# A transformer layer on one core: the residual stream moves from SBUF to the output in DRAM, and four of five down-projection parts are added to it by accumulating transfers

## The chip, the cores and the metric

The kernel runs on one core of a Trainium2 chip, in float32. Its engines work side by side, each through its own queue in order: TensorE (PE, with its weight loads as PEld), VectorE (DVE), ScalarE (ACT), GpSimd (POOL) and SyncE (SP), which here only issues transfers. The metric is the time of one execution on the device, in microseconds. Before the change it is 1356.28 us, the median of three runs (1355.2 to 1356.44).

## The reference

The kernel computes one encoder layer for 256 tokens of 2048 channels. What matters here is its second half:

```python
    x = x + (g[:, :, 0] * y_a + g[:, :, 1] * y_b) @ w_o

    gt, up = jnp.split(rms_norm(x, g_ffn) @ w_gate_up, 2, axis=-1)
    return x + (jax.nn.silu(gt) * up) @ w_down
```

The first line adds the attention branches to the residual stream `x`. The last one adds the feed-forward network (FFN) to it; its inner width is 5632. The result, 256 x 2048 float32 (2 MB), is the output.

## The kernel before

Every weight is read once from DRAM, in chunks. A chunk in the FFN is 1 MB, loaded by two transfers of 512 KB from SP's queue into one of three buffers (`x`, pool `xp`). It is split into two float32r parts: ACT casts it (`wh`, L220) and DVE subtracts the cast from the original (`wl`, L221). `wh` and `wl` live in six buffers, so three chunks of the FFN. PE then makes three products for each pair of tiles (`mm3`, L427 to L429). SP's next load into an `x` buffer waits until DVE has made `wl` of the chunk that held it; ACT's next cast waits until PE has freed a `wh` buffer. So a delay of one load can travel round this ring: load, cast, subtraction, next load.

The FFN goes by five parts of the inner width (`PARTS`, L40), numbered 0 to 4; the first has three column groups of 512, the others two. In each part:

- **Gate and up.** A column group takes eight chunks (`Quad`). Three of the eight are "fast" (L837): DVE and ACT make extra splits and sums of them (`rh`, `rl`, `r`, and the four additions L844 to L847, which write into the `x` buffer before its own cast and subtraction), and PE then needs seven products where it would need eight. At a group's end DVE collects four PSUM banks, A to D (`evac_fast` L658, `evac_pair` L670; L679 is the step that PE waits for before it writes bank C again).
- **Down.** Four column blocks of 512, j = 0 to 3, each 256 x 512, collected in the banks A, B, C and A. Blocks 0 and 1 run interleaved, then 2 and 3. When a block is complete, `evac_down` (L701) adds it to the residual tile `x1[j]`.

`x1[0]` to `x1[3]` are SBUF tiles of [128, 2, 512] float32 (512 KB each), made by `evac_wo` (L637) as the sum of the attention projection and the input. They are held from there to the end, 28 buffers of this size (pool `tp`) being shared with all other tiles of that size. After part 4 each goes to the output by one transfer from SP; the last block, j = 3, by halves and quarters as its rows are done (`evac_last`, L708).

The order of all instructions is written out by hand as far as the second block of `w_o`. From `ffn_at - 2` (L981) a list scheduler orders each engine's queue by the order of the code as a priority and its own costs. Functions registered with `at(group, fn, ahead)` (L932) run some steps ahead of that group's first product; `load_xres` is one.

Weight chunks are numbered through the program: 253 to 260 are the eight of part 1's first group; 255, 257 and 259 are its fast ones.

Of the kernel before, what the change touches and what calls it, by code (L numbers as in the profile page):

```python
# [15 lines left out]
ALU = mybir.AluOpType  # L16
# [3 lines left out]
P = 128  # L20
S = 256
NT = S // P
# [17 lines left out]
PARTS = ((0, 3), (3, 5), (5, 7), (7, 9), (9, 11))  # L40
# [55 lines left out]
def layer_kernel(ctx: ExitStack, tc: tile.TileContext, a: dict, out: bass.AP):  # L96
    nc = tc.nc
# [11 lines left out]
    def t4(shape, name, dt=F32):  # L109
        return tp.tile(shape, dt, name=name, tag="t4")  # L110

    def small(shape, name):
        return cp.tile(shape, F32, name=name)
# [30 lines left out]
    od = out[0].rearrange("(t p) d -> p t d", p=P)  # L144
# [50 lines left out]
    def rstd_of(ss, d, name):  # L195
        n = math.prod(ss.shape[1:])
        v = small(list(ss.shape), name + "_v")
        r = small(list(ss.shape), name)
        nc.gpsimd.tensor_scalar(v, ss, 1.0 / d, EPS, op0=ALU.mult, op1=ALU.add)
        flat = (lambda z: z) if len(ss.shape) == 2 else (lambda z: z.rearrange("p a b -> p (a b)"))  # L200
        nc.gpsimd.tensor_tensor(flat(r), flat(v), mhalf[:, :n], op=ALU.pow)
        return r
# [401 lines left out]
    x1, hP, hjobs, xres = {}, {}, {}, {}  # L604
    ss2 = small([P, NT, 4], "ss2")

    def load_xres(j):
        xres[j] = t4([P, NT, 512], f"xres{j}")
        nc.sync.dma_start(xres[j], xd[:, :, j * 512:(j + 1) * 512])
# [3 lines left out]
    def job_h(i):  # L613

        ps = half_side(f"tr_h{i}").rearrange("p (k s) -> p k s", s=S)
        for k in range(2):
            f = 2 * i + k
            for t in range(NT):
                nc.tensor.transpose(ps[:, k, t * P:(t + 1) * P], x1[f // 4][:, t, (f % 4) * P:(f % 4 + 1) * P], ident)
        g = [gain("g_ffn", 2 * i + k) for k in range(2)]  # L620
        if i not in FAST:
            hP[i] = t4([P, 2, 2, S], f"hP{i}", F32R)
            split_evac(*((hP[i][:, 0, k], hP[i][:, 1, k], ps[:, k], g[k]) for k in range(2)))
        else:
            v, l, h = t4([P, 8, P], f"hs{i}"), t4([P, 7, P], f"hsl{i}", F32R), t4([P, 7, P], f"hsh{i}", F32R)
            nc.scalar.activation(v[:, 0:8:7], ps[:, 0].rearrange("p (t s) -> p t s", t=NT), AF.Copy, scale=g[0])
            nc.scalar.activation(v[:, 1:3], ps[:, 1].rearrange("p (t s) -> p t s", t=NT), AF.Copy, scale=g[1])
            nc.vector.tensor_sub(v[:, 3], v[:, 7], v[:, 2])
            nc.vector.tensor_sub(v[:, 4], v[:, 7], v[:, 0])
            nc.vector.tensor_sub(v[:, 5], v[:, 0], v[:, 3])  # L630
            nc.vector.tensor_sub(v[:, 6], v[:, 1], v[:, 5])
            split_pair(h, l, v[:, :7])
            hq[i] = (h, l)
        return
        yield

    def evac_wo(j):  # L637
        def evac(ps, step):
            x1[j] = t4([P, NT, 512], f"x1_{j}")
            nc.vector.tensor_add(x1[j], ps, xres[j])  # L640
            sq = t4([P, NT, 512], f"sq1_{j}")
            for t in range(NT):
                nc.scalar.activation(sq[:, t], x1[j][:, t], AF.Square, accum_out=ss2[:, t, j:j + 1])

            for i in (2 * j, 2 * j + 1):
                hjobs[i] = Job(job_h(i))
                hjobs[i].ready = step + 2
                jobs.append(hjobs[i])
            if j == 3:
                s = small([P, NT], "ss2s")  # L650
                nc.vector.tensor_reduce(s, ss2, axis=AX.X, op=ALU.add)
                st["2"] = rstd_of(s, DM, "r2")
        return evac
# [46 lines left out]

    def evac_down(half, j):  # L701
        def evac(ps, step):
            nc.vector.tensor_add(x1[j], ps, x1[j])
            if half == len(PARTS) - 1:
                nc.sync.dma_start(od[:, :, j * 512:(j + 1) * 512], x1[j])
        return evac

    def evac_last(ps, t):  # L708
        for c in range(t + 1):
            w = 512 // (t + 1)  # L710
            s = slice(w * c, w * (c + 1))
            nc.vector.tensor_add(x1[3][:, t, s], ps[:, s], x1[3][:, t, s])
            (nc.scalar if c else nc.sync).dma_start(od[:, t, 1536 + w * c:1536 + w * (c + 1)], x1[3][:, t, s])
# [41 lines left out]
    for half, (j0, j1) in enumerate(PARTS):  # L755
        js = range(j0, j1)
        hidT[half] = Act(f"hid{half}", 4 * len(js))
        for i, j in enumerate(js):
            needs = {k: (lambda k=k: [hjobs[k]]) for k in range(NPAIR)}
            needs[FAST[0]] = lambda: list(hjobs.values())  # L760
            if i:
                needs[FAST[0]] = lambda half=half, i=i: [djobs[half, i - 1]]
            groups.append(Group(W["w_gate_up"], 512 * j, 1024, range(NPAIR), None, evac_pair(half, i, i == len(js) - 1), needs))
        for j in range(4):
            wd = W["w_down"][js[0] * 512:(js[-1] + 1) * 512]
            groups.append(Group(wd, 512 * j, 512, range(4 * len(js)), hidT[half], evac_down(half, j),
                                {k: (lambda k=k, half=half: [djobs[half, k // 4]]) for k in range(4 * len(js))}))
# [126 lines left out]
    def products(i):  # L894
        c, ks, first, last = steps[i]
        g, gi, allks, q = chunks[c]
        if q:
            return products_quad(c)
        final = gi == len(groups) - 1
        if first and gi < ffn_at:  # L900
            ps = psm.tile([P, NT, 512], F32, name=f"g{gi}", tag="main")
            gps[gi] = [ps, ps[:, 0], ps[:, 1]]
        elif first:
            ps = held[DOWN[g.c0 // 512]]
            gps[gi] = [ps, ps[:, 0], ps[:, 1]]
        ps = gps[gi]
        h, l = parts[c]
        if ks[-1] == allks[-1]:
            del parts[c]

        def products_of(t, k):
            ah, al = g.lhs(k)
            n, s = k - allks[0], slice(t * P, (t + 1) * P)
            mm3(ps[1 + t][:, :g.n], ah[:, s], al[:, s], h[:, n, :g.n], l[:, n, :g.n], k == g.ks[0], k == g.ks[-1])

        if final and last:
            for t in range(NT):
                for k in ks:
                    products_of(t, k)
                evac_last(ps[1 + t], t)  # L920
        else:
            for k in ks:
                for t in range(NT):
                    products_of(t, k)
        return ps[0]
# [3 lines left out]
    def gidx(fn_name, nth=0):  # L929
        return [i for i, n in enumerate(names) if f".{fn_name}." in n][nth]  # L930

    def at(gi, fn, ahead=8):  # L932
        early.setdefault(max(0, first_step[gi] - ahead), []).append(fn)
# [9 lines left out]
    for j in range(4):  # L943
        at(gidx("evac_g0", j), lambda j=j: load_bias(j))
        at(gidx("evac_g1", j), lambda j=j: load_bias(4 + j))
        at(gidx("evac_wo", j), lambda j=j: load_xres(j))

    after_evac = {}
    after_evac[gidx("evac_b", 0)] = lambda: jobs.append(prep["kr"])
    after_evac[gidx("evac_b", 6)] = lambda: limited.extend(attn["dil", p] for p in range(4))  # L950
# [28 lines left out]
    for i, (c, ks, first, last) in enumerate(steps):  # L979
# [18 lines left out]
        ps = products(i)  # L998
# [61 lines left out]
```

## Time and profile before

| | us |
|---|---|
| median of three runs | 1356.28 |
| the profiled execution, its own time | 1356.11 |
| its span (first to last instruction) | 1354.3 |
| time outside the span | 1.8 |

The profile is taken from one execution on the core. Its page gives busy times of the engines, the chain of work that ended last, and groups of equal instructions. A row of the timeline gives start, duration, engine, line, operation, what it writes and reads with its shape, and in brackets the idle time of the engine before it and what ended that. The stages by the clock of this trace: attention and its projections up to about 640 us; part 0 of the FFN to 830; parts 1 to 4 about 130 us each, with gate and up first and the down blocks in the last 43 us of each; the end at 1354.

### The profile page before, as it was taken

Reading aid. Unit: us, or ns where it says so; the run is one execution under the profiler, and the core shown is the slowest. Engines: PE = TensorE matmul, PEld = TensorE weight load, DVE = VectorE, ACT = ScalarE, POOL = GpSimd, SP = SyncE. Lnnn points to the kernel's source line nnn. Section 1 sums busy time; section 2 is a strip of 40 time slices with the busy share of each in tenths; the row PEclk is TensorE's granted clock in tenths of the full one; section 3 lists DMA queues with packets and bytes.
Section 4 is the critical chain, followed back from the end, with each engine's and each line's share of the span. In section 5 each row is a group of like instructions: output and inputs, shape, how many; then the busy total and the mean of one; then the engine's idle time right before and its main releaser. Section 6 shows DMA issues by size and latency. Waiting matters only on the chain.

```text
span 1354.3 us, 16169 instructions
## 1 busy us (share of the span) xinstructions
PE 1339.5 (99%) x6243; PEld 1126.0 (83%) x6243; DVE 949.1 (70%) x949; ACT 652.2 (48%) x724; POOL 34.3 (3%) x41
## 2 busy tenths in 40 slices
PE   8999999999999999999999999999999999999998
PEld 6899999988888888888788888888878888888886
DVE  5566777677645655567789756886798579857973
ACT  6455555454444444455455434454445345534541
POOL 1011112000000000000000000000000000000000
PEclk9999999999999999999999999999999999999999
DMA  7555555656556766676546665565457654754662
GB/s 247 179 175 161 161 170 167 184 161 176 174 186 205 212 188 202 209 235 207 201 158 213 221 187 183 191 213 190 157 185 245 191 186 172 229 190 163 214 214 93
DMA packets 138205, 257.14 MB, mean 190 GB/s; under 512 B 9192, under 2 KB 28688, under 8 KB 138128
## 3 DMA queue, kind: packets, MB, share of 16 engines
q1 hardware_dynamic: 137760, 255.96, 58.9%
q8 instruction: 49, 0.80, 0.2%
q14 instruction: 28, 0.23, 0.1%
q10 hardware_dynamic: 144, 0.13, 0.0%
q0 software_dynamic: 224, 0.01, 0.0%
HBM read 253.97 MB, written 2.10 MB: 189 GB/s over the span
## 4 chain that ended last, share of the span: by engine, by line
PE 94%; DVE 2%; issue 1%; DMA 1%; ACT 1%; SPq 0%; DVEq 0%; ACTq 0%
PE g L429 14%; PE g L427 14%; PE g L428 13%; PE sC L427 6%; PE sC L429 6%; PE sC L428 6%; PE mA L427 4%; PE mA L429 4%; PE mA L428 4%; PE sD L429 4%; PE sD L427 4%; PE sD L428 4%; PE mB L428 3%; PE mB L429 3%; PE mB L427 3%
## 5 line engine op out<-in xcount | busy, mean ns | idle before, releaser
L220 ACT CAST wh<-x 128x1024 fp32r<-128x1024 f32 (+3 forms) x349 | 465.3, 1352 | 437.0 <-DVE x L847 127.7
L221 DVE TENSOR_TENSOR wl<-x,wh 128x2048 fp32r<-128x2048 f32 x132 | 300.8, 2289 | 134.5 <-ACT wh L220 132.7
L221 DVE TENSOR_TENSOR wh<-x,wh 128x1024 fp32r<-128x1024 f32 (+2 forms) x217 | 250.6, 1172 | 113.1 <-ACT wh L220 111.9
L427 PE MATMUL g<-wh,xTh 128*128 128x512 f32 (+1 forms) x544 | 210.6, 387 | 0.6 <-ACT xTh L212 0.6
L429 PE MATMUL g<-wh,xTl 128*128 128x512 f32 (+1 forms) x544 | 207.9, 382 | 0.6 <-DVE xTl L217 0.6
L428 PE MATMUL g<-wh,xTh 128*128 128x512 f32 (+1 forms) x544 | 207.9, 382 | 0.0
L429 PEld LDWEIGHTS g<-wh,xTl 128*128 128x128 f32 x544 | 102.8, 189 | 17.6 <-DVE xTl L217 1.4
L427 PEld LDWEIGHTS g<-wh,xTh 128*128 128x128 f32 x544 | 102.8, 189 | 15.9 <-ACT xTh L212 0.9
L428 PEld LDWEIGHTS g<-wh,xTh 128*128 128x128 f32 x544 | 102.9, 189 | 15.4 <-DVE wh L221 0.4
L427 PE MATMUL sC<-wh,hP 128*128 128x512 f32 x220 | 86.1, 391 | 1.6 <-DVE u L679 1.5
L429 PE MATMUL sC<-wh,hP 128*128 128x512 f32 x220 | 85.7, 390 | 0.0
L429 PE MATMUL sD<-wh,hP 128*128 128x512 f32 x220 | 85.7, 389 | 0.0
L428 PE MATMUL sC<-wl,hP 128*128 128x512 f32 x220 | 85.7, 389 | 0.0
L427 PE MATMUL sD<-wh,hP 128*128 128x512 f32 x220 | 85.7, 389 | 0.0
L428 PE MATMUL sD<-wl,hP 128*128 128x512 f32 x220 | 85.7, 389 | 0.0
L220 ACT CAST rh<-x 128x1024 fp32r<-128x1024 f32 x33 | 34.7, 1051 | 36.1 <-DMA x<-in_w_gate_up_dram 36.1
L427 PEld LDWEIGHTS sC<-wh,hP 128*128 128x128 f32 x220 | 41.3, 188 | 12.3 <-issue 4.0
L427 PE MATMUL g<-wh,mTh 128*128 128x512 f32 x128 | 50.5, 394 | 0.0
L429 PE MATMUL g<-wh,mTl 128*128 128x512 f32 x128 | 49.9, 390 | 0.0
L428 PE MATMUL g<-wh,mTh 128*128 128x512 f32 x128 | 49.9, 390 | 0.0
L427 PEld LDWEIGHTS sD<-wh,hP 128*128 128x128 f32 x220 | 41.3, 188 | 8.6
L428 PEld LDWEIGHTS sD<-wl,hP 128*128 128x128 f32 x220 | 41.3, 188 | 8.6
(675 smaller groups left out, 2390.7 us busy)
## 6 DMA issues: line engine op xcount, KB each, us to landing
x<-in_w_gate_up_dram SPq DMA_DIRECT2D x176, 512.0 KB, 4.7
x<-in_w_down_dram SPq DMA_DIRECT2D x88, 512.0 KB, 5.0
x<-in_w_in_dram SPq DMA_DIRECT2D x79, 512.0 KB, 4.2
x<-in_w_in_dram SPq DMA_DIRECT2D x56, 448.0 KB, 3.6
x<-in_w_o_dram SPq DMA_DIRECT2D x32, 512.0 KB, 4.4
x<-in_w_o_mla_dram SPq DMA_DIRECT2D x16, 512.0 KB, 4.9
x<-in_w_o_dil_dram SPq DMA_DIRECT2D x16, 512.0 KB, 4.6
x<-in_w_ukv_dram SPq DMA_DIRECT2D x8, 512.0 KB, 4.0
```

Of the source, the lines that this page charges most:

```text
L220: nc.scalar.copy(h, x)
L221: nc.vector.tensor_sub(l, x, f32(h))
L427: nc.tensor.matmul(ps, ah, bh, start=first, stop=False)
L428: nc.tensor.matmul(ps, ah, bl, start=False, stop=False)
L429: nc.tensor.matmul(ps, al, bh, start=False, stop=last)
```

## The change

The residual stream is stored to the output in DRAM as soon as it is made. In the parts 0 to 3, ACT copies a finished down block from PSUM to a new SBUF tile `y`, and a transfer issued by POOL adds that tile to the output's columns in DRAM (`accum_op=ALU.add`). For part 4, the sum so far is read back from the output into new tiles `x1[j]` two steps ahead of each block's first product; the addition on DVE and the store are then as before.

```diff
@@ evac_wo
             for t in range(NT):
                 nc.scalar.activation(sq[:, t], x1[j][:, t], AF.Square, accum_out=ss2[:, t, j:j + 1])
 
+            nc.sync.dma_start(od[:, :, j * 512:(j + 1) * 512], x1[j])
             for i in (2 * j, 2 * j + 1):
@@ evac_down
         def evac(ps, step):
-            nc.vector.tensor_add(x1[j], ps, x1[j])
-            if half == len(PARTS) - 1:
-                nc.sync.dma_start(od[:, :, j * 512:(j + 1) * 512], x1[j])
+            cols = od[:, :, j * 512:(j + 1) * 512]
+            if half < len(PARTS) - 1:
+                y = t4([P, NT, 512], f"y{half}_{j}")
+                nc.scalar.copy(y, ps)
+                nc.gpsimd.dma_start(cols, y, accum_op=ALU.add)
+            else:
+                nc.vector.tensor_add(x1[j], ps, x1[j])
+                nc.sync.dma_start(cols, x1[j])
         return evac
+
+    def load_x1(j):
+        x1[j] = t4([P, NT, 512], f"x1b_{j}")
+        nc.sync.dma_start(x1[j], od[:, :, j * 512:(j + 1) * 512])
...
+    for j in range(4):
+        at(gidx("evac_down", 4 * (len(PARTS) - 1) + j), lambda j=j: load_x1(j), 2)
```

In the changed kernel the new lines are 645 (store of `x1`), 707 and 708 (copy and accumulating transfer), 710 and 711 (addition and store of part 4), 716 (read back); the four additions L844 to L847 stand at L854 to L857.

The scheduler also moves some instructions. On PE nothing moves but three products of part 0's first group, by a few places each. On ACT and DVE the same thing happens at the start of each of the parts 1 to 4. First ACT, where part 0's last down blocks meet part 1's first chunks, before:

```order
L220 CAST wh252_6303<-x252_6245 128x2048
L220 CAST wh253_6334<-x253_6276 128x2048
L220 CAST rh255_6366<-x255_6338 128x1024
L220 CAST r255_6368<-x255_6338 128x512
L220 CAST wh254_6377<-x254_6307 128x2048
L220 CAST wh255_6409<-x255_6338 128x2048
L220 CAST rh257_6440<-x257_6413 128x1024
L220 CAST wh256_6451<-x256_6381 128x2048
```

and in the change:

```order
L220 CAST wh253_6342<-x253_6284 128x2048
L220 CAST wh254_6387<-x254_6315 128x2048
L707 COPY y0_2_6373<-sC_5121 128x1024
L220 CAST rh255_6376<-x255_6346 128x1024
L220 CAST r255_6378<-x255_6346 128x512
L707 COPY y0_3_6418<-mA_5119 128x1024
L220 CAST wh255_6421<-x255_6346 128x2048
L220 CAST rh257_6452<-x257_6425 128x1024
L220 CAST wh256_6463<-x256_6391 128x2048
L220 CAST r257_6454<-x257_6425 128x512
```

Two copies have come in, and the cast of chunk 254 now stands ahead of the first two casts of chunk 255. DVE at the same place, before (`sC` and `mA` are the banks with the blocks 2 and 3):

```order
L221 TENSOR_TENSOR wl253_6335<-x253_6276,wh253_6334 128x2048
L221 TENSOR_TENSOR rl255_6367<-x255_6338,rh255_6366 128x1024
L703 TENSOR_TENSOR x1_2_4917<-sC_5117,x1_2_4917 128x1024
L221 TENSOR_TENSOR r255_6368<-x255_6338,r255_6368 128x512
L221 TENSOR_TENSOR wl254_6378<-x254_6307,wh254_6377 128x2048
L844 TENSOR_TENSOR x255_6338<-x255_6338 128x512
L845 TENSOR_TENSOR x255_6338<-x255_6338 128x512
L703 TENSOR_TENSOR x1_3_5097<-mA_5115,x1_3_5097 128x1024
L846 TENSOR_TENSOR x255_6338<-x255_6338 128x512
L847 TENSOR_TENSOR x255_6338<-x255_6338 128x512
L221 TENSOR_TENSOR wl255_6410<-x255_6338,wh255_6409 128x2048
```

and in the change:

```order
L221 TENSOR_TENSOR wl253_6343<-x253_6284,wh253_6342 128x2048
L221 TENSOR_TENSOR wl254_6388<-x254_6315,wh254_6387 128x2048
L221 TENSOR_TENSOR rl255_6377<-x255_6346,rh255_6376 128x1024
L221 TENSOR_TENSOR r255_6378<-x255_6346,r255_6378 128x512
L854 TENSOR_TENSOR x255_6346<-x255_6346 128x512
L855 TENSOR_TENSOR x255_6346<-x255_6346 128x512
L856 TENSOR_TENSOR x255_6346<-x255_6346 128x512
L857 TENSOR_TENSOR x255_6346<-x255_6346 128x512
L221 TENSOR_TENSOR wl255_6422<-x255_6346,wh255_6421 128x2048
```

The two additions are gone, and the subtraction of chunk 254 (`wl254`) has moved ahead of the two of chunk 255 (`rl255`, `r255`). On SP's queue, where part 4's down weights begin, stood before:

```order
L826 DMA x339_9335<-in_w_gate_up_dram 128x2x512 x2
L826 DMA x340_9374<-in_w_gate_up_dram 128x2x512 x2
L835 DMA x341_9405<-in_w_down_dram 128x2x512 x2
L835 DMA x342_9433<-in_w_down_dram 128x2x512 x2
L835 DMA x343_9464<-in_w_down_dram 128x2x512 x2
L835 DMA x344_9499<-in_w_down_dram 128x2x512 x2
L835 DMA x345_9538<-in_w_down_dram 128x2x512 x2
```

and now:

```order
L836 DMA x340_9410<-in_w_gate_up_dram 128x2x512 x2
L716 DMA x1b_0_9496<-out_0_dram 128x2x512
L845 DMA x341_9441<-in_w_down_dram 128x2x512 x2
L845 DMA x342_9469<-in_w_down_dram 128x2x512 x2
L845 DMA x343_9502<-in_w_down_dram 128x2x512 x2
L845 DMA x344_9537<-in_w_down_dram 128x2x512 x2
L716 DMA x1b_1_9572<-out_0_dram 128x2x512
L845 DMA x345_9578<-in_w_down_dram 128x2x512 x2
```

Each read back stands between two weight loads, and waits there for the accumulating transfers into its columns.

## The prediction

> **What bounds the kernel now.** I read the page's first and fourth parts, then the waits of PE alone from 640 us on (the FFN), then one window.
>
> ```profile
> PE 1339.5 (99%) x6243; PEld 1126.0 (83%) x6243; DVE 949.1 (70%) x949; ACT 652.2 (48%) x724; POOL 34.3 (3%) x41
> PE 94%; DVE 2%; issue 1%; DMA 1%; ACT 1%; SPq 0%; DVEq 0%; ACTq 0%
> ...
> PE sD L691 <- DVE z L685: 1.7, 2, 1.0
> PE sC L427 <- DVE u L679: 1.5, 5, 0.9
> PE mA L619 <- ACT hs L627: 0.9, 1, 0.9
> PE mA L427 <- DVE x L712: 0.8, 1, 0.8
> ...
> 520.00:640.00 120.00, 120.00 (x551) 99.59 (x550) 76.11 (x78) 60.31 (x77) 0.00 (x0) 1.00 0.65 214
> ```
>
> PE is busy for 99% of the span and carries 94% of the last chain. In the whole FFN its waits sum to 4.9 us, and between 520 and 640 us, where the residual is made, it is busy in all 120.00 us. The change takes no matmul away. So the forecast starts from 1356.11 us, the profiled execution's own time (0.17 us under the median of the runs shown, which is nothing beside the terms below). To gain, the change must remove one of these waits; to lose, it must make a new one.
>
> **The change part by part.** The 16 additions of parts 0 to 3 leave DVE, and 16 copies of the same shape come to ACT.
>
> ```profile
> L703 DVE TENSOR_TENSOR x<-mA,x 128x1024 f32<-128x1024 f32 x9 | 11.0, 1221 | 7.0 <-PE mA L429 7.0
> L210 ACT CAST hid1h<-sD 128x1024 fp32r<-128x1024 f32 x1 | 1.0, 1018 | 0.3 <-PE sD L691 0.3
> ```
>
> DVE loses 16 x 1.22 = 19.5 us. ACT, by its nearest row (the same shape from PSUM, 1.02 us), gains 16.3 us. Both engines have room (70% and 48%), so both terms are nothing by themselves. What counts is where they stand in the ring of loads and splits. Two places differ.
>
> *In the middle of a down phase* the ring has much room:
>
> ```profile
> 944.20 1.91 ACT L220 CAST wh<-x 128x2048 fp32r<-128x2048 f32 x1 [3.53 <-PE sC L428]
> 949.64 1.91 ACT L220 CAST wh<-x 128x2048 fp32r<-128x2048 f32 x1 [3.53 <-PE mA L428]
> 951.59 2.29 DVE L221 TENSOR_TENSOR wl<-x,wh 128x2048 fp32r<-128x2048 f32 x1 [3.15 <-ACT wh L220]
> ```
>
> ACT stands 3.53 us of each 5.44 us until PE frees a buffer. With three chunks' buffers the freed one is needed two chunks later, 10.9 us, and the split takes 1.91 + 2.29 = 4.2 us: 6.7 us to spare. The copies of blocks 0 and 1 (1.02 us) and whatever their transfers do to one load hide there. The bank is not wanted back for two chunks either. Cost 0; it would be the excess of a delay over 6.7 us.
>
> *At the start of parts 1 to 4* the ring has little. DVE, then ACT, where part 1 begins:
>
> ```profile
> 825.99 1.22 DVE L703 TENSOR_TENSOR x<-sC,x 128x1024 f32<-128x1024 f32 x1
> 827.12 0.68 DVE L221 TENSOR_TENSOR r<-x,r 128x512 fp32r<-128x512 f32 x1
> 827.72 2.28 DVE L221 TENSOR_TENSOR wl<-x,wh 128x2048 fp32r<-128x2048 f32 x1
> ...
> 831.25 1.22 DVE L703 TENSOR_TENSOR x<-mA,x 128x1024 f32<-128x1024 f32 x1
> ...
> 833.10 0.69 DVE L847 TENSOR_TENSOR x<-x 128x512 f32<-128x512 f32 x1
> ...
> 825.24 1.91 ACT L220 CAST wh<-x 128x2048 fp32r<-128x2048 f32 x1
> 833.90 1.91 ACT L220 CAST wh<-x 128x2048 fp32r<-128x2048 f32 x1 [6.75 <-DVE x L847]
> 835.72 1.04 ACT L220 CAST rh<-x 128x1024 fp32r<-128x1024 f32 x1
> ```
>
> The chain is: the additions L844 to L847 on chunk 255, the cast of it at 833.90, then `rh` of chunk 257. Taking both L703 out looks like a gain of 2.4 us, but the new order gives it back. ACT casts chunk 254 at 825.24 as now (it waits for PE's buffer), to 827.15; then the copy of block 2 to 828.1, `rh255` to 829.1, `r255` to 829.6. DVE makes `wl254` first, 827.2 to 829.46, then `rl255` (1.22) and `r255` (0.68) to 831.2, then four additions at 0.72 us apart, to 834.17. Before they end at 833.10 + 0.69 = 833.79. The chain is 0.37 us later. The copy of block 3 waits for PE; even if it began only when the addition did, at 831.25, it would be over at 832.3, ahead of the cast that comes behind it at 834.27.
>
> Now the loads. Two rows of SP and, under each, the landing times (minimum, median, maximum) of its two transfers: chunk 257 in part 1, and the same chunk one part later.
>
> ```profile
> 830.03 1.20 SPq L826 DMA_DIRECT2D x<-in_w_gate_up_dram  x2
> DMA to landing us min/median/max: 4.3/4.6/5.0
> ...
> 960.06 1.19 SPq L826 DMA_DIRECT2D x<-in_w_gate_up_dram  x2
> DMA to landing us min/median/max: 4.1/5.1/6.2
> ```
>
> And from the timeline what came of it: the start of the subtraction of chunk 256 in part 1, the cast of the third chunk and that same subtraction in part 2, and PE's first product behind L679 at the end of the first group, in both parts.
>
> ```profile
> 839.79 2.29 DVE L221 TENSOR_TENSOR wl<-x,wh 128x2048 fp32r<-128x2048 f32 x1
> 963.93 1.91 ACT L220 CAST wh<-x 128x2048 fp32r<-128x2048 f32 x1 [6.76 <-DVE x L847]
> 970.88 2.28 DVE L221 TENSOR_TENSOR wl<-x,wh 128x2048 fp32r<-128x2048 f32 x1
> 872.31 0.47 PE L427 MATMUL sC<-wh,hP 128*128 128x512 f32 x1 [0.16 <-DVE u L679]
> 1003.08 0.47 PE L427 MATMUL sC<-wh,hP 128*128 128x512 f32 x1 [0.89 <-DVE u L679]
> ```
>
> This is an experiment that the trace made by itself. The parts are 963.93 - 833.90 = 130.03 us apart. In part 2 the second transfer landed 1.2 us late. The subtraction some steps on starts at 970.88 where 839.79 + 130.03 = 969.82 was due: the ring is 1.06 us late. It does not recover, for at the group's end PE waits 0.89 us for L679 and not 0.16: 0.73 us lost. So a ring that is late by L costs PE about L - 0.33 there.
>
> The load of chunk 257 is the one that the accumulating transfers meet. It is issued behind `wl254`, now at about 829.5 (829.46 where it was 830.0), and lands at 835.06; its first cast starts at 836.1, behind the cast of 255, so 1.04 us of delay D is free. Blocks 2 and 3 are handed to POOL at about 828.1 and 832, so one of them, or parts of both, shares the DMA engines with it. Hence
>
> cost of one part's start = 0.37 + max(0, D - 1.04) - 0.33.
>
> The trace shows no accumulating transfer. The nearest row is that of the plain ones; beside it the only kind of issue that POOL makes:
>
> ```profile
> q1 hardware_dynamic: 137760, 255.96, 58.9%
> L163 POOL DMA_DIRECT2D grow<-in_g_ffn_dram x1: 484/484/484, 4.7 to 4.7; - x1
> ```
>
> 58.9% of 1354.3 us for 255.96 MB is 1.63 us of all 16 engines for 0.524 MB. In the pair at 830.03 the second transfer, 0.6 us behind, lands 5.0 - 4.3 + 0.6 = 1.3 us after the first. So a plain one takes 1.3 to 1.6 us of the engines from its neighbour. [...] I take D = 1.5 us, one plain transfer, the value nearest to a row. Then a start costs 0.50 us, four cost 2.0 us; with D = 0 it is 4 x 0.04 = 0.2 us, with D = 3.2 it is 4 x 2.2 = 8.8 us. POOL is idle there, and its issue (0.48 us for one small transfer) delays nothing but the transfer.
>
> [...]
>
> *Stores of `x1`, and the reading back.* A store stands in SP's queue behind a wait for L640:
>
> ```profile
> 566.75 1.23 DVE L640 TENSOR_TENSOR x<-g,xres 128x1024 f32<-128x1024 f32 x1 [2.24 <-PE g L429]
> 564.54 7.40 SPq L835 DMA_DIRECT2D x<-in_w_o_dram  x2
> 573.36 1.05 ACT L220 CAST wh<-x 128x1024 fp32r<-128x1024 f32 x1
> ...
> 1280.95 1.20 SPq L826 DMA_DIRECT2D x<-in_w_gate_up_dram  x2
> 1284.70 0.89 SPq L835 DMA_DIRECT2D x<-in_w_down_dram  x2
> L427 PE MATMUL mB<-wh,hid3h x16: 389/389/475, 1182.0 to 1197.8; 128*128 128x512 f32 x16
> ```
>
> For the first block SP now stands to 568.0, with an input tile and the load of 564.54 queued behind. That load goes out some 4.4 us late and lands at about 574.3; its cast started at 573.36. So at most 0.9 us of delay on a stage in which PE has not waited once: cost 0, bound 0.9. The other three come just before a wait for DVE that lasts longer. The reading back stands at about 1282.2, between two loads of which the second waits for DVE until 1284.70. Part 3's block 1 ends near 1198, blocks 2 and 3 four chunks of 5.44 us later, at 1220: the last accumulating transfer has 62 us to land. Cost 0. The end (last addition, last store) is unchanged.
>
> Sum: 1356.11 + 2.0 = **1358.1 us**.
>
> **The rivals.**
>
> *The accumulating transfer is dear.* If it costs its neighbour two plain ones, D = 3.0 and a start costs 2.0 us: 1356.11 + 8.0 = 1364.1, slower. It decides from D = 1.7 us on, where four starts cost 2.8 us. For it: the free 1.04 us is small, and two transfers fall within 4 us. Against: the load's data and theirs may miss each other. [...]
>
> *DVE's relief reaches PE.* If every wait for DVE in the FFN ahead of the end vanished, 1.7 + 1.5 us would go: 1352.9. Against: the two L691 waits come at the start of the down phase, 90 us after the last addition, and four of the five L679 waits are 0.2 us or less.
>
> *The read back holds SP.* If an accumulating transfer took more than 62 us, SP would stand, with every weight load of part 4's down phase behind it, and each further microsecond beyond the 6.7 to spare would be lost. Against: a plain 512 KB lands in 5 us.
>
> **How the numbers follow.** A measurement of this kernel can tell about 0.2% (2.7 us) from no change. Forecast, D between 0 and 1.7: 0.56, within 0.2%. Dear transfers: 0.38, slower. Relief: 0.04, faster. SP held: 0.02, slower. The range goes from 1355.4, which allows the forecast's lower end (1356.3) about the spread of the runs shown, to 1356.11 + 8.8 = 1364.9, the upper bound of D.
>
> **What would show it.** Copies on ACT of about 1.02 us; in the four starts the load of the fifth chunk landing D later than 5.0 us, and the cast of the third chunk 0.37 us later against PE; the wait of PE for L679 grown from 1.5 us to about 3.5 (forecast) or over 9 (dear). If PE's new waits stand elsewhere, in the down phases or behind the read back, the reasoning on the ring is wrong. If D is over 1.7 us and PE does not wait, the step L - 0.33 is wrong.

## The result and the profile after

| | before | after |
|---|---|---|
| median, us | 1356.53 (1355.2 to 1360.68, 6 runs) | 1370.35 (1367.01 to 1373.79, 6 runs) |
| ratio | | 1.0097, 95% interval 1.0076 to 1.0118 |
| profiled execution, its own time / span, us | 1356.11 / 1354.3 | 1367.01 / 1365.2 |

The change costs about 1%, more than the forecast (1358.1 us) and more than the upper end of its range (1364.9). The profiled execution of after is the fastest of its six; its span is 10.9 us longer than that of before.

The page of after, its line of busy times (us, share of the span, instructions):

```profile
PE 1340.0 (98%) x6243; PEld 1125.5 (82%) x6243; DVE 931.1 (68%) x933; ACT 667.0 (49%) x740; POOL 53.4 (4%) x57
```

PE does the same work in the same busy time (1340.0 against 1339.5 us), so all 10.9 us are waits or a slower start behind them. DVE is 18.0 us lighter and ACT 14.8 us heavier, about as worked out (19.5 and 16.3); neither shows in the time. The waits of PE from 640 us on in after (total, times, longest; L680, L684 and L692 are the lines L679, L683 and L691 of before):

```profile
PE mA L619 <- ACT hs L627: 4.6, 1, 4.6
PE sC L427 <- ACT z L684: 3.2, 2, 2.1
PE sC L427 <- DVE u L680: 3.2, 3, 1.8
PE mA L428 <- DVE wl L221: 1.2, 2, 0.7
PE mA L427 <- DVE x1b L722: 0.8, 1, 0.8
```

Two places grew. The wait for `hs` at L619 went from 0.9 to 4.6 us: +3.7. The wait for the group's end before bank C is written (L427, the second and third row; the two name different steps, on ACT and on DVE, of the same collection) went from 1.5 to 6.4 us, and a wait for `wl` came with it: +4.9 and +1.2. The wait at L691 for DVE's L685, 1.7 us before, is gone. The last row, for the read back tiles, is as before.

*First place: 649 us, where the FFN begins.* Windows of after, two stretches: the wait, and what follows it (length, PE busy and count, then the other engines, the granted clock, the DMA share and GB/s):

```profile
649.60:654.30 4.70, 0.14 (x1) 0.00 (x0) 2.65 (x4) 2.64 (x3) 0.00 (x0) 0.99 0.57 180
654.30:658.00 3.70, 3.67 (x12) 3.12 (x13) 2.60 (x6) 1.12 (x2) 0.00 (x0) 0.55 0.30 82
```

PE stands 4.6 us. Then its clock is granted at 0.55 for 3.7 us: twelve products in 3.67 us. With the n-th product of after set against the n-th product of before, PE is 4.6 us late as the wait ends and 5.8 us late when the clock is back. The place costs about 5 us in all (3.7 + 1.2).

*Second place: the starts of parts 1 to 4.* From the timeline of after, PE's first product behind the collection of each part's first group (in before the idle times were 0.16, 0.89, 0.16 and 0.16 us):

```profile
879.00 0.47 PE L427 MATMUL sC<-wh,hP 128*128 128x512 f32 x1 [1.07 <-ACT z L684]
1010.74 0.47 PE L427 MATMUL sC<-wh,hP 128*128 128x512 f32 x1 [1.82 <-DVE u L680]
1141.16 0.47 PE L427 MATMUL sC<-wh,hP 128*128 128x512 f32 x1 [1.22 <-DVE u L680]
1272.85 0.47 PE L427 MATMUL sC<-wh,hP 128*128 128x512 f32 x1 [2.15 <-ACT z L684]
```

All four are late. The load that was to be late is late, too. From the timeline of after, at the start of part 4, the two transfers of the last blocks on POOL and, between them, the load of the fifth chunk on SP:

```profile
1225.85 1.19 POOL L708 DMA_DIRECT2D out_dram<-y  x1 [15.12 <-ACT y L707]
1229.72 1.19 POOL L708 DMA_DIRECT2D out_dram<-y  x1 [2.68 <-ACT y L707]
...
1227.00 1.23 SPq L836 DMA_DIRECT2D x<-in_w_gate_up_dram  x2
```

What the view of that load's line gives for its two transfers from issue to landing:

```profile
DMA to landing us min/median/max: 6.6/7.7/8.8
```

In before, the same load in the timeline, and below it the same line of the view by source line:

```profile
1219.74 1.20 SPq L826 DMA_DIRECT2D x<-in_w_gate_up_dram  x2
DMA to landing us min/median/max: 4.0/4.4/4.7
```

The last half lands 8.8 instead of 4.7 us after its issue. The difference is what the prediction calls D, here 4.1 us. In parts 1 to 3 it is, by the same subtraction, 2.7, 3.1 and 3.1 us (mean of the four 3.25).

The account, before against after: +3.7 and +1.2 at 649 us, +4.9 and +1.2 in the parts' first groups, -1.7 at L691, and +0.9 us, a wait for the first transposes of `x1` near 595 us that before does not have. That is 10.2 of the 10.9 us.

The profiled execution is 3.3 us under the median of its six, and the clocks on record point to where the rest lies. Its mean granted clock is 0.998; the other five have 0.995 to 0.997. By an estimate from these figures (the share of the clock that is missing, times the span) they lose 1.4 to 4.1 us more to stretches of lower clock; they are 2.2 to 6.8 us longer.

### The profile page after: what moved, and what is told of

Read it like the earlier page. It is cut to its first block, busy times and chain, and to the rows that moved or that the text cites. A ratio compares the mean times of both kernels' runs of the same rounds, so it can differ in the third digit from the quotient of the medians.

```text
span 1365.2 us, 16245 instructions
## 1 busy us (share of the span) xinstructions
PE 1340.0 (98%) x6243; PEld 1125.5 (82%) x6243; DVE 931.1 (68%) x933; ACT 667.0 (49%) x740; POOL 53.4 (4%) x57
## 4 chain that ended last, share of the span: by engine, by line
PE 81%; DMA 7%; DVE 6%; ACT 3%; issue 3%; SPq 0%; DVEq 0%; ACTq 0%
PE g L429 12%; PE g L427 12%; PE g L428 12%; PE sC L427 5%; PE sC L428 5%; PE sC L429 5%; DMA x<-in_w_gate_up_dram 4%; PE mA L427 3%; PE mA L429 3%; PE mA L428 3%; ACT wh L220 3%; PE sD L428 3%; PE sD L427 3%; PE sD L429 3%; DMA x<-in_w_o_dram 3%
## 5 line engine op out<-in xcount | busy, mean ns | idle before, releaser
L427 PE MATMUL g<-wh,xTh 128*128 128x512 f32 (+1 forms) x544 | 210.0, 386 | 2.1 <-ACT xTh L212 2.1
L427 PEld LDWEIGHTS g<-wh,xTh 128*128 128x128 f32 x544 | 102.5, 188 | 17.4 <-ACT xTh L212 2.4
L427 PE MATMUL sC<-wh,hP 128*128 128x512 f32 x220 | 86.1, 391 | 6.5 <-ACT z L684 3.2
L427 PE MATMUL sD<-wh,hP 128*128 128x512 f32 x220 | 85.8, 390 | 0.0
L427 PEld LDWEIGHTS sC<-wh,hP 128*128 128x128 f32 x220 | 41.3, 188 | 17.3 <-issue 8.9
L427 PE MATMUL g<-wh,mTh 128*128 128x512 f32 x128 | 50.5, 394 | 0.0
L427 PEld LDWEIGHTS sD<-wh,hP 128*128 128x128 f32 x220 | 41.6, 189 | 8.7
L429 PEld LDWEIGHTS sD<-wh,hP 128*128 128x128 f32 x220 | 41.4, 188 | 8.6
```

The lines of the kernel that those rows point to most:

```text
L427: nc.tensor.matmul(ps, ah, bh, start=first, stop=False)
L429: nc.tensor.matmul(ps, al, bh, start=False, stop=last)
```

## The experiments

All ratios are against the kernel before, run on the same chip in the same rounds (1358.71, 1358.26 and 1359.52 us for the three sets).

| what runs | median, us | ratio, 95% interval |
|---|---|---|
| stores only | 1362.05 | 1.0028 (1.0016 to 1.0041) |
| accumulating transfers only, input stored early | 1367.39 | 1.0065 (1.0048 to 1.0082) |
| after without accumulating transfers | 1362.29 | 1.0026 (1.0015 to 1.0037) |
| after with plain transfers from POOL | 1362.02 | 1.0025 (1.0012 to 1.0038) |
| stores only, from POOL | 1361.58 | 1.0024 (1.0012 to 1.0036) |
| stores only, 2 KB each | 1357.39 | 0.9993 (0.9982 to 1.0004) |
| after, blocks 0 and 1 accumulated only | 1361.86 | 1.0031 (1.0019 to 1.0043) |
| no stores, transfers held to the first group's end | 1373.50 | 1.0112 (1.0099 to 1.0125) |
| no stores, those of blocks 2 and 3 held to the down part | 1357.78 | 0.9986 (0.9972 to 1.0000) |
| no stores, blocks 0 and 1 only | 1361.33 | 1.0011 (0.9997 to 1.0025) |
| after with two plain transfers for each one | 1365.66 | 1.0038 (1.0022 to 1.0054) |

### Which part of the change costs

Stores alone: before, with

```diff
+            nc.sync.dma_start(od[:, :, j * 512:(j + 1) * 512], x1[j])
             for i in (2 * j, 2 * j + 1):
```

> The kernel before with only the four stores of x1 added in evac_wo (SP's queue, as in the change); the additions stay on DVE and nothing accumulates. Theory A (two causes: the stores make the ring of loads and splits late by 4.8 us, which PE meets at its first transposes into bank A at 649 us; the accumulating transfers cost the four part starts the rest): PE waits 4 to 5 us for ACT hs L627 near 650 us and runs about 1 us slower behind it; 1360 to 1363 us, and no other PE wait over 1 us. Rival B (the accumulating transfers are all of it, the stores only happen to stand near): within 0.2% of before, 1354 to 1359 us.

Measured 1.0028. The first row of its waits:

```profile
PE mA L619 <- ACT hs L627: 3.7, 1, 3.7
```

And the window behind that wait, with the granted clock 0.59 third from the end:

```profile
653.50:657.50 4.00, 3.95 (x13) 3.17 (x14) 2.91 (x6) 1.40 (x3) 0.00 (x0) 0.59 0.32 95
```

The wait at 649 us and the lower clock behind it (0.59 over 4.0 us) come with the stores alone, in a kernel that has no accumulating transfer. Two other waits of this trace are over 1 us, more than was expected: 1.5 us for bank C in part 2 and 1.2 us at L692.

The other way round, no stores in `evac_wo`, but an output that something is accumulated on:

```diff
+            if which == "cq":
+                for c in range(4):
+                    nc.gpsimd.dma_start(od[:, :, c * 512:(c + 1) * 512], xn[c])
...
-            nc.sync.dma_start(od[:, :, j * 512:(j + 1) * 512], x1[j])
```

> The change, but the output first receives the input tiles (by POOL's queue, at the end of the first projection) in place of the four stores of x1 in evac_wo; the attention branches are so left out of the residual that part 4 adds. Theory A: the wait of 4.6 us at 649 us is gone, the waits at the four part starts stay: 1361 to 1367 us. Rival B: as the change, 1368 to 1372 us.

Measured 1.0065, with the waits at the starts of the parts as in after (6.8 us in all before bank C). The two parts add up: 0.28 + 0.65 = 0.93% of 0.97%. The split is not quite clean, as this trace still has a wait of 2.0 us at the place of 649 us, where before has 0.9. It also shows what the profiled execution of after happens not to: behind two of the four starts PE's clock falls (granted 0.63 and 0.59 in the 4.6 and 4.2 us behind waits of 2.2 and 2.0 us), which costs another 1.3 and 1.4 us, product against product with before.

Then after without the transfers, and with plain ones:

```diff
-                nc.gpsimd.dma_start(cols, y, accum_op=ALU.add)
```

> The change without the 16 accumulating transfers: the copies on ACT stay, parts 0 to 3 are left out of the output. Theory A: only the stores' loss is left, 1360 to 1363 us, with PE's waits at the part starts back at 0.2 us. Rival C (the copies in ACT's queue, and the new order of the splits there, cost the part starts, not the transfers): 1366 to 1371 us with the waits for L679's counterpart as in the change.

```diff
-                nc.gpsimd.dma_start(cols, y, accum_op=ALU.add)
+                nc.gpsimd.dma_start(cols, y)
```

> The change with 16 plain transfers from POOL's queue in place of the accumulating ones (parts 0 to 3 overwrite one another in the output and are not summed). Theory A with accumulating transfers worth two plain ones: the load of a start's fifth chunk is late by about half of the 2.7 to 4.1 us that it is late in the change, four starts cost 1 to 3 us, 1362 to 1365 us. Rival D (any transfer of POOL's queue costs the same, adding or not): as the change, 1368 to 1372 us.

1.0026 and 1.0025: both are at what the stores cost. The copies on ACT, the new order and the reading back show no cost, and neither do sixteen plain transfers of 512 KB at the very same places, for which a cost of 1 to 3 us had been expected. The waits of PE with plain transfers:

```profile
PE mA L619 <- ACT hs L627: 4.1, 1, 4.1
PE sD L692 <- DVE z L686: 1.5, 2, 0.8
PE sC L427 <- DVE u L680: 1.4, 4, 0.7
```

The group's end is at 1.4 us again (1.5 in before). The load of part 4's fifth chunk, issued at 1225.95 us here, by the view of its line:

```profile
DMA to landing us min/median/max: 4.5/5.3/6.0
```

It lands 6.0 - 4.7 = 1.3 us later, of which the prediction had 1.04 us as free; in parts 1 to 3 it is 0.7, 0.2 and 1.2 us. POOL's queue on the DMA page (packets, MB, share of 16 engines' span), in after and then with plain transfers:

```profile
q0 software_dynamic: 4576, 8.40, 4.1%
```

```profile
q0 software_dynamic: 2528, 8.40, 1.7%
```

The same 8.40 MB take 1.7% of the engines' span and 2528 packets, where accumulating takes 4.1% and 4576. That is 0.017 x 1361.7 / 16 = 1.45 us of all 16 engines for a plain transfer and 0.041 x 1365.2 / 16 = 3.5 us for an accumulating one.

### Is it the time on the DMA engines?

```diff
-                nc.gpsimd.dma_start(cols, y, accum_op=ALU.add)
+                nc.gpsimd.dma_start(cols, y)
+                nc.gpsimd.dma_start(od[:, :, (j + 2) % 4 * 512:((j + 2) % 4 + 1) * 512], y)
```

> Changed kernel with two plain transfers of POOL in place of each accumulating one, the second of y to the block two further on (parts 0 to 3 are left out of the result). Theory G (what costs at a part's start is the time that the transfers take of the 16 engines: 3.5 us for an accumulating one, 1.45 for a plain one, about 2.9 for two): the load of the fifth chunk lands 2 us late or more, ratio 1.005 to 1.009. Rival K (it is the accumulating kind itself, that is reading the output and adding): ratio 1.002 to 1.004 as with one plain transfer.

Measured 1.0038: below what theory G gave and inside what K gave, but with an interval that reaches both. The trace says more than the time. The load of part 4's fifth chunk (issued at 1226.98 us):

```profile
DMA to landing us min/median/max: 5.7/6.5/7.3
```

POOL's queue:

```profile
q0 software_dynamic: 4832, 16.79, 3.4%
```

And the rows for bank C among PE's waits from 640 us on:

```profile
PE sC L427 <- DVE u L680: 2.9, 3, 1.7
PE sC L427 <- ACT z L684: 1.6, 1, 1.6
```

The load lands 7.3 - 4.7 = 2.6 us late, between 1.3 (one plain transfer, 1.45 us of the engines) and 4.1 (accumulating, 3.5 us). In parts 1 to 3 it is 1.9, 2.5 and 2.0 us, and the means of the four starts are 0.85, 2.25 and 3.25 us. The waits before bank C are 4.5 us, between 1.4 and 6.4. So two plain transfers, 2.9 us of the engines, bring the load more than half of the way from the one to the other.

In time they bring less: 0.13% over one plain transfer (1.0038 against 1.0025), where accumulating brings 0.72% (1.0097). The intervals are wide, but at their ends the two plain ones come to about 0.3% and accumulating to about 0.5%. So the time on the engines explains the direction and more than half of the delay. Whether the accumulating kind costs the neighbours something beyond it, as the times suggest, or whether the longer delays are dearer for another reason, such as the lower clock behind some of PE's waits (0.63 and 0.59 in the run with the input stored early), is not settled by this run.

### Does the place matter?

After, with blocks 2 and 3 kept in `x1` as before:

```diff
-            if half < len(PARTS) - 1:
+            if half < len(PARTS) - 1 and j < 2:
                 y = t4([P, NT, 512], f"y{half}_{j}")
                 nc.scalar.copy(y, ps)
                 nc.gpsimd.dma_start(cols, y, accum_op=ALU.add)
...
-    for j in range(4):
+    for j in range(2):
         at(gidx("evac_down", 4 * (len(PARTS) - 1) + j), lambda j=j: load_x1(j), 2)
```

> Changed kernel with column blocks 0 and 1 added to the output by accumulating transfers as there, and blocks 2 and 3 added by DVE into x1 as before (and stored at the end). Theory A1 (an accumulating transfer costs where it stands in the way of the loads of the next part's first group; blocks 2 and 3 end right ahead of it, blocks 0 and 1 stand in the middle of the down part, where PE has over 6 us to spare): the part starts go back to before within 0.3 us each, the stores remain, ratio 1.002 to 1.004. Rival A2 (each accumulating transfer costs its share wherever it stands): half of the starts' 0.65%, ratio 1.0055 to 1.0075.

Measured 1.0031, the price of the stores, with the starts of the parts back (waits of PE from 640 us on):

```profile
PE mA L619 <- ACT hs L627: 3.6, 1, 3.6
PE sC L427 <- DVE u L680: 1.0, 4, 0.5
...
PE sD L692 <- DVE z L686: 0.3, 1, 0.3
```

Eight accumulating transfers in the middle of the down parts cost nothing that shows. The price is that of the last two of each part, which meet the next part's first loads.

### What about the stores costs: SP that stands still, or the bytes?

Before with stores at the same places, once from POOL's queue, once from SP's with one row of 2 KB:

```diff
+            nc.gpsimd.dma_start(od[:, :, j * 512:(j + 1) * 512], x1[j])
```

> Kernel of before with the four stores of x1 in evac_wo, issued from POOL's queue, so that SP is not held until x1 is there; output as the reference's. Theory S (the stores cost 0.28% because SP, which issues the weight loads in order, stands still at each store): the loads go out as before, no wait of more than 1.5 us for mA L619 / hs L627, ratio 0.999 to 1.001. Theory T (they cost it because 512 KB of writes share the 16 DMA engines with the loads): the wait stays above 2.5 us, ratio 1.002 to 1.004. I take S with 0.6.

```diff
+            nc.sync.dma_start(od[0:1, 0:1, j * 512:(j + 1) * 512], x1[j][0:1, 0:1])
```

> Kernel of before with four stores at the same places on SP's queue, each of one row of 2 KB only, so that SP waits for x1 as with the full stores and almost nothing is written. Theory S (SP held): the first load behind the first store still goes out some 4 us later, the wait for mA L619 / hs L627 is 2.5 us or more, ratio 1.002 to 1.004. Theory T (512 KB of writes): the loads land within 1.5 us of their old distance to the step, wait under 1.5 us, ratio 0.999 to 1.001. A share of both shows as a ratio of 1.001 to 1.002 here and in the run with POOL's queue.

I had given theory S 0.6; it fell. With the bytes but without the hold the ratio is 1.0024; with the hold but without the bytes, 0.9993. SP's queue in three traces, the rows around the first store (start, duration of the group of issues): before, stores from POOL, stores of 2 KB.

```profile
564.54 24.16 SPq L835 DMA_DIRECT2D x<-in_w_o_dram  x10
```

```profile
564.05 25.06 SPq L836 DMA_DIRECT2D x<-in_w_o_dram  x10
```

```profile
567.71 0.32 SPq L645 DMA_DIRECT2D out_dram<-x  x1
568.08 0.39 SPq L609 DMA_DIRECT2D xres<-in_x_dram  x1
568.57 21.14 SPq L836 DMA_DIRECT2D x<-in_w_o_dram  x10
```

With 2 KB the loads behind the first store do go out 4.0 us late, and nothing comes of it. What comes of the bytes shows 70 us later. The cast of chunk 220, one of the FFN's first, on ACT: before, after, stores from POOL, stores of 2 KB.

```profile
640.24 1.92 ACT L220 CAST wh<-x 128x2048 fp32r<-128x2048 f32 x1
```

```profile
645.03 1.91 ACT L220 CAST wh<-x 128x2048 fp32r<-128x2048 f32 x1
```

```profile
642.54 1.91 ACT L220 CAST wh<-x 128x2048 fp32r<-128x2048 f32 x1
```

```profile
640.95 1.91 ACT L220 CAST wh<-x 128x2048 fp32r<-128x2048 f32 x1
```

The ring of loads and casts is 4.8 us late in after, 2.3 with POOL's stores and 0.7 with the tiny ones, and PE's wait for `hs`, which ACT makes behind the next such cast (6.6 us on, as late as this one), is 4.6, 3.2 and 1.9 us. Between 566 and 650 us the transfers take 67% of the DMA engines in before (71% in after). The window of before, DMA share second from the end:

```profile
566.00:650.00 84.00, 83.15 (x384) 68.64 (x382) 56.52 (x61) 45.90 (x62) 2.12 (x2) 1.00 0.67 220
```

The stage has room on average, and yet the ring doesn't make up for what the stores displace in it, as each load goes out only when an earlier chunk has been split. PE's stock shrinks by itself towards the end of the stage: in before, chunk 215 was split 12.0 us ahead of its first product and chunk 219 only 6.0 us; in after the latter had 2.0 us. The step from late loads to no recovery is read from these numbers, not tried by itself.

One caution. The place at 649 us is on an edge and varies from one execution to the next: the third version of the last section below, which has no store there, shows a wait of 3.0 us at it in its profile, and the runs of before on that chip go from 1354.8 to 1365.4 us. That the stores cost 0.24 to 0.31% rests on the rounds of five kernels, not on one trace.

### A version without the two costs

The first: no stores in `evac_wo`; part 0 is added on DVE and stored by plain transfers; the accumulating ones are held back.

```diff
-            nc.sync.dma_start(od[:, :, j * 512:(j + 1) * 512], x1[j])
...
-            if half < len(PARTS) - 1:
+            if half == 0:
+                nc.vector.tensor_add(x1[j], ps, x1[j])
+                nc.gpsimd.dma_start(cols, x1[j])
+            elif half < len(PARTS) - 1:
                 y = t4([P, NT, 512], f"y{half}_{j}")
                 nc.scalar.copy(y, ps)
-                nc.gpsimd.dma_start(cols, y, accum_op=ALU.add)
+                late.append((cols, y))
... in evac_pair, behind the step that makes z
+            while late:
+                cols, y = late.pop(0)
+                nc.vector.scalar_tensor_tensor(y[:, 0, :1], z[:, 0, :1], 0.0, y[:, 0, :1], op0=ALU.mult, op1=ALU.add)
+                nc.gpsimd.dma_start(cols, y, accum_op=ALU.add)
```

> A mended version, output as the reference's: no stores in evac_wo; part 0 is added by DVE into x1 and stored by plain transfers of POOL (which cost nothing at the part's start in the run with plain transfers); parts 1 to 3 are copied to y and added by accumulating transfers as in the changed kernel, but each transfer is held back until the first group of the next part has been evacuated (a one-column DVE step on y, which reads that group's z, stands between). Theory A (stores at one place, transfers beside the part's first loads): both costs gone, ratio 0.999 to 1.002. Rival: transfers in the middle of a part meet loads that are just as close, and y's buffers held 50 us longer hold others up: ratio 1.004 or more.

Measured 1.0112, no better than the change itself. The four largest of its waits from 640 us on:

```profile
PE mA L428 <- DVE wl L221: 5.5, 3, 1.8
PE sD L695 <- DVE z L685: 3.1, 3, 1.5
PE sD L428 <- DVE wl L221: 3.0, 3, 1.3
PE mA L619 <- ACT hs L627: 1.9, 1, 1.9
...
```

POOL's timeline in part 2, four issues behind one another:

```profile
1010.99 4.91 POOL L689 DMA_DIRECT2D out_dram<-y  x4 [174.91 <-ACT r L220]
```

And a window right behind them:

```profile
1020.00:1030.00 10.00, 10.00 (x46) 8.29 (x45) 3.94 (x3) 2.75 (x2) 0.00 (x0) 1.00 1.08 305
```

The place of the stores is better (1.9 us there, 4.6 in after). But four transfers in a row fill the DMA engines (share 1.08; four times 3.5 us = 14 us) in the middle of a part, and in each of three parts PE waits for splits that come late (5.5 and 3.0 us). So gate and up seems to have little to spare all along, not only at its start. This run changes two things at once, the place and the bunching of four, and does not tell them apart. The buffers of `y` are held longer, too; the next version holds two of them longer still, at no cost that shows.

The second holds only blocks 2 and 3, and to the last group's end, where the down part begins (cut against the first):

```diff
+                if j < 2:
+                    nc.gpsimd.dma_start(cols, y, accum_op=ALU.add)
+                else:
+                    late.append((cols, y))
...
-            while late:
+            while last and late:
```

> Second mended version, output as the reference's: no stores in evac_wo; part 0 is added by DVE into x1 and stored by plain transfers of POOL; in parts 1 to 3 blocks 0 and 1 are added by accumulating transfers at once, and those of blocks 2 and 3 are held back until the last group of the next part has been evacuated, which is the start of its down part. Theory A1 (accumulating transfers are free in a down part's first half and in its middle, and cost at the first group of a part or where four of them follow one another beside close loads): ratio 0.999 to 1.002. Rival A3 (the down parts' loads are as close as those of the pairs, and blocks 0 and 1 were free only because POOL and the rings had nothing else): 1.003 or more.

Measured 0.9986 (0.9972 to 1.0000): the output of the change, at the time of before. Its waits from 640 us on:

```profile
PE sC L427 <- DVE u L679: 2.5, 4, 1.1
PE mA L619 <- ACT hs L627: 1.2, 1, 1.2
PE mA L427 <- DVE x1b L731: 0.8, 1, 0.8
PE sD L695 <- DVE z L685: 0.6, 1, 0.6
```

POOL's queue there:

```profile
q0 software_dynamic: 4064, 8.40, 3.3%
```

Twelve accumulating transfers and 3.3% of the DMA engines are still there; only where they run has changed. It is not faster by more than the measurement can tell.

The third is half of it: blocks 0 and 1 as there, blocks 2 and 3 in `x1` from beginning to end.

> Half of the change, output as the reference's: no stores in evac_wo; block 0 and 1 leave SBUF after part 0 (added by DVE, stored by plain transfers of POOL), are added to by accumulating transfers in parts 1 to 3 and read back for part 4; blocks 2 and 3 stay in x1 as before. Both costs are left out, so 0.999 to 1.001. If something of the change that was not yet named costs too, it is above 1.002.

Measured 1.0011 (0.9997 to 1.0025), at the edge of what was expected; the interval neither shows nor excludes a small third cost. Its profiled execution (span 1363.9 us) is the slowest of its twelve. It has the wait of 3.0 us at L619 spoken of above, and these before bank C:

```profile
PE sC L427 <- DVE u L679: 2.9, 3, 2.0
PE sC L427 <- ACT z L683: 2.5, 2, 1.7
```

That is 5.4 us, nearly the 6.4 of after, though no accumulating transfer stands at the start of a part here, and the fifth chunk's load lands 4.6, 6.2, 4.6 and 4.4 us after its issue, about as in before. So these waits can be some 4 us longer in one execution without the transfers, for a reason that stays open. That the transfers cost the parts' starts rests on the medians (1.0097 and 1.0065 with them there, 1.0024 to 1.0031 for the five kernels that have the stores and none of them there) and on the late loads, not on the waits of one trace.

## Why the prediction was wrong

*The step that failed: "Stores of `x1`", cost 0, bound 0.9.* It measured 0.24 to 0.31%, 3.3 to 4.2 us. Three things in it were wrong. It priced what SP's hold does to the first load behind it, and that hold is harmless, as the run with 2 KB stores showed. It left out the 2 MB of writes, which take about 1.45 us of all engines each from the loads, by the run with plain transfers, although the part on the accumulating transfers used just this price. And it took "a stage in which PE has not waited once" for a stage with room. PE worked off a stock of split chunks there; the stock was smaller at the end, and the one row of waits for ACT that the prediction quotes (`hs`, 0.9 us, at 649 us) was the sign that nothing is left there: a place where PE already waits passes on every further delay. The lower clock behind the wait (granted 0.55 over 3.7 us in after, 0.50 over 4.9 us with plain transfers), some 1.2 to 2.6 us in these runs, comes on top; before has no such stretch in the FFN from which it could have been read (granted 1.00 from 640 us on).

*The term that was mis-sized: D.* Taken as 1.5 us, one plain transfer; it measured 2.7 to 4.1 us, mean 3.25. The upper end, twice a plain one or 3.2 us, and the rival with D = 3.0 had the size. No run shows the factor of two that both rest on; in POOL's queue the accumulating kind took 3.5 / 1.45 = 2.4 times the engine time of a plain one.

*What held.* The place: the load of the fifth chunk, at all four starts, and PE's wait for the collection of the banks. The plain transfer's D of 1.5 with 1.04 us free, as the most that a plain one does: with plain transfers D came out at 0.2 to 1.3 us and the starts cost nothing. The middle of the down part: no cost, with 6.7 us to spare. The copies, DVE's relief, the reading back: nothing that shows, each as forecast. The new order's 0.37 us came out smaller: in part 1 the cast of the third chunk is 5.89 us later than in before (839.79 against 833.90 us) and PE 5.8 us, which leaves 0.1.

*The formula of a start.* With the measured D it gives the sum of D - 1.0 over four starts, 9.0 us. The waits in the profiled execution of after come to half of that, 4.9 + 1.2 - 1.7 = 4.4 us. The 1.7 us are waits for L691 that before had further on; a PE that comes later to them no longer waits. By the medians, the accumulating transfers cost 0.65% (without the stores) to 0.72% (against plain ones), 8.8 to 9.8 us. That is near the formula, but in part by luck: the medians also hold the lower clock behind some of the waits (0.63 and 0.59 in the run with the input stored early), of which the formula knows nothing.

So the dear rival's 1364.1 us plus 3.3 to 4.2 us for the stores makes 1367.4 to 1368.3, beside 1367.01 for the profiled execution and 1370.35 for the median.

## What to carry to other kernels

An engine that never waits in a stage proves nothing about its stock: look for the next place where it does wait, however little, and ask whether traffic added earlier is made up for by then. Price an accumulating transfer at least by the time that it takes of the DMA engines, about 2.4 plain ones here, and ask where it lands among the loads: accumulating transfers cost 0.7% with two of them at each part's start, over 1% with four in a row in the middle of gate and up, and nothing that shows beside the down products. And when traces of single executions differ by as much as the effect, let the medians decide. Before moving traffic to a "quiet" time, check which loads are close there.

## What the runs showed of the hardware

*PE at a lower clock after a wait.* In the thirteen traces, from 100 us on, PE stood 3.0 us or longer at L619 in eight (3.0, 3.2, 3.6, 3.7, 3.9, 4.1, 4.2 and 4.6 us), and each time 5 to 12 of the next products ran about 0.4 us apart instead of 0.23, 1.2 to 2.6 us lost. The granted clock behind five of the eight: 0.61 over 4.1 us (wait of 3.0), 0.50 over 4.2 us (3.2), 0.59 over 4.0 us (3.7), 0.50 over 4.9 us (4.1) and 0.55 over 3.7 us (4.6). Of eleven waits between 1.8 and 2.2 us, five had the same after-effect (0.63 and 0.59 behind 2.2 and 2.0 us in the run with the input stored early) and six had not (1.00 behind 2.15 and 1.82 us in after). Behind the shorter ones in before, up to 1.0 us, the clock was 1.00. One of the mild cases, stores of 2 KB, a wait of 1.85 us up to 650.2:

```profile
650.20:654.00 3.80, 3.75 (x19) 3.18 (x20) 2.70 (x6) 1.19 (x2) 0.00 (x0) 1.00 0.34 93
```

Nineteen products in 3.75 us at clock 1.00, where after had twelve in 3.67 us at 0.55. The slow stretches differ in length: in after the products are 0.23 us apart again from 657.74 us on (the wait ended at 654.33); in the run with plain transfers the clock is 0.86 from 649 to 655.1 us and still 0.50 from there to 660. What sets the length, and which of the waits of about 2 us are followed by one, the traces do not show. So a wait of 3 us or more at L619 cost 1.2 to 2.6 us more than itself.

*The accumulating kind.* Per 512 KB: 1.2 us of POOL for the issue and 6.5 us to landing; plain 0.73 and 3.7 us. The rows for POOL's issues (count, busy, mean ns), after and the run with plain transfers:

```profile
L708 POOL DMA_DIRECT2D out_dram<-y x16 | 19.1, 1197 | 564.6 <-ACT y L707 564.6
```

```profile
L708 POOL DMA_DIRECT2D out_dram<-y x16 | 11.7, 734 | 569.9 <-ACT y L707 569.9
```
